# The long convolutions of a hybrid encoder layer: a new order of work, filters through DRAM, an unsplit second stage

## The chip, the cores and the metric

The kernel runs on one core of a Trainium2 chip. A core has TensorE (PE, matmuls), VectorE (DVE), ScalarE (ACT), GpSimd (POOL) and SyncE (SP), which issues most transfers; sixteen DMA engines move data between DRAM and the on-chip SBUF (128 partitions); matmuls write to PSUM, whose banks DVE and ACT empty. The metric is the time of one execution in microseconds of the device, as the median of several runs.

## The reference

One encoder layer on 2048 tokens of 1024 channels, float32. A projection feeds two mixers: a gated long convolution (512 channels) and an RWKV-7 recurrence (512 channels). Their outputs are projected, gated, merged and normed; a SwiGLU network and a second norm follow. What the change touches is the long convolution:

```
u = short_conv3(u, conv_w, conv_b)          # three taps along the tokens
v, x1, x2 = split(u, 3)
h = hyena_filters(L, ...)                   # (L, 2 orders, 2 directions, 512): small network x decaying window
z = x1 * long_conv(v, h[:, 0, 0], h[:, 0, 1], skip[0])
z = x2 * long_conv(z, h[:, 1, 0], h[:, 1, 1], skip[1])

def long_conv(z, h_fwd, h_bwd, d_skip):     # by FFT of length 2L = 4096
    hf = rfft(h_fwd) + conj(rfft(h_bwd))
    return irfft(rfft(z) * hf)[:L] + z * d_skip
```

## The kernel before, in words

The stages follow each other: projection with preparation of the recurrence, the recurrence in 64 steps (`chain`), the convolutions (`hyena`), the merge (`merge`) and the feed-forward network (`ffn`). A scheduler at build time puts each engine's instructions in order by priorities and costs; inside a block under `manual_schedule` the engines named there keep the order of the program. In `chain` and `hyena` of the kernel before only PE is named.

The FFT is done with matmuls against constant matrices, in two stages, for four tiles of 128 channels (index c), twice per tile (order o = 0, 1): eight convolutions i = 2c + o. The steps, with their lines:

- Short convolution (`short`, lines 1166 to 1172): for each 512 tokens one load, one ACT step and two DVE steps. Three per tile: v, x1, x2.
- `turned` (1240): PE transposes of the result to tokens on partitions, copied by ACT.
- `fwd` (1254): the first FFT stage of the data; ACT copies the PSUM tiles into U (1256).
- `flip` (1221): four DVE transposes of 32 x 32 blocks turn U into V, which the second stage needs whole.
- The filters (`filt`): 32 windows (ACT exponentials, 1200), matmuls with the small network's last layer (1201), DVE product with the window (1205), the first FFT stage (1191), an ACT copy (1192), then also a `flip`. The filter of one convolution has 16 matmul pieces, 8 of line 1201 and 8 of line 1191; they are drawn from a generator between other work (`pull`).
- `product`: for q = 0 to 7 the second stage of the filter (`load`, 1275; ACT copy 1281; the two halves swapped by four small SP transfers, 1285), the second stage of the data (`step3`), two DVE products with the filter's spectrum (1312, 1313) and the way back (1297, 1298), copied by ACT (1299). For q above 0 `parts` first splits the data into a high and a low float32r part (ACT 197, DVE 198), and `step3` makes three 512-column matmuls (202 to 204) instead of four fp32 ones.
- After a product: `flip`, `inverse` (1327), for o = 0 a DVE product with x1 (1389) and `fwd` again; for o = 1 `finish`: inverse, ACT copy (1344), PE transposes (1336), DVE product with x2 (1338), a store to `yhd` (1354).

PE in program order goes through tile c as: transposes of x1, finish of tile c - 1, product o = 0 with pieces of the next filter between its rounds, the rest of those pieces, inverse and forward, transposes for tile c + 1, product o = 1, forward of tile c + 1. The first pieces are made at the end of the recurrence, in its last two steps and between its last four small parts. The merge's first half block (`right`) is computed around the last `finish`, after its weights are split.

Of the kernel before, what the change touches and what calls it, by code (L numbers as in the profile page):

```python
# [9 lines left out]
F32 = mybir.dt.float32  # L10
F32R = mybir.dt.float32r
# [178 lines left out]
class Layer:  # L190
# [38 lines left out]
    def build(self):  # L229
        tc, nc = self.tc, self.nc  # L230
        with tc.tile_pool(name="dr", bufs=1, space=DRAM) as dr, tc.tile_pool(name="keep", bufs=1, reuse_waits="tile") as keep:
# [8 lines left out]
            self.Yd = T("Yd", [NCH, P, 256])  # L240
            self.Nd, self.Wd = T("Nd", [2, P, 1024]), T("Wd", [2, P, 1024])
# [377 lines left out]
    def ring(self, k, n=512):  # L619
        return self.cm.tile([P, 514], F32, name="rg", tag=f"rg{k % 14}")[:, 0:n]  # L620

    def chain(self):
# [3 lines left out]
        with tc.tile_pool(name="ch", bufs=1, reuse_waits="tile") as s, tc.tile_pool(name="chp", bufs=1, space=PSUM, reuse_waits="tile") as ps:  # L626
# [166 lines left out]
            def step(n):  # L793
# [16 lines left out]
                if n + 2 < N:  # L810
                    fetch(n + 2)
# [132 lines left out]

            LAST = N - 3
# [81 lines left out]
            with tc.manual_schedule(engines={mybir.EngineType.PE}):  # L1027
# [17 lines left out]
                taps, pieces = iter(()), [1, 2, 3]  # L1045
                self.rush = 0
                for n in range(N):
# [5 lines left out]
                    if n == LAST + 1:  # L1053
                        taps = self.filt(0, 0)
                    if n >= LAST + 1:
                        aux.append(self.part(taps, 4.0))
                        cost += 4.0
# [6 lines left out]
                    if n == LAST:  # L1064
                        self.open()
# [16 lines left out]
                self.taps = taps  # L1082
# [8 lines left out]
    def part(self, gen, need):  # L1091
        while need > 0:
            t = next(gen, None)
            if t is None:
                return
            need -= t
            yield t


    def open(self):  # L1100
# [3 lines left out]
        cu = self.wp.tile([P, 1024], F32, name="cu0", tag="wraw", bufs=2)  # L1104
# [3 lines left out]
        self.turns = dict(cu=0, row=0, w=0, g=0, A=0, B=0, H=0, Hs=0)  # L1108
        self.smalls, self.Vfs = {}, {}
# [6 lines left out]
        self.cus = [cu, self.ring(13, 514)]  # L1116
        self.z0 = self.short(0, True)
# [12 lines left out]
    def next(self, name):  # L1130
        first, n = dict(w=(8, 2), g=(10, 2), A=(12, 2), B=(0, 2), H=(2, 3), Hs=(5, 3))[name]
# [15 lines left out]
    def row(self):  # L1147
        self.turns["row"] += 1
        return self.cm.tile([P, L], F32, name="co", tag=f"X{1 - self.turns['row'] % 2}")


    def short(self, ct, byrest):
        nc, cw, cb = self.nc, self.cw, self.cb
        stt = nc.vector.scalar_tensor_tensor
        o = self.row()
        for b in range(NB):
            u = self.cus[self.turns["cu"] % 2]
            self.turns["cu"] += 1
# [5 lines left out]
            nc.sync.dma_start(u[:, lo:hi], self.ud[ct, :, 512 * b - 1 + lo:512 * b - 1 + hi])  # L1164
            t = self.wp.tile([P, 512], F32, name="cv", tag="ev", bufs=2) if byrest else o[:, 512 * b:512 * b + 512]
# [7 lines left out]
        return o  # L1173

    def pre(self, k):
        return self.cm.tile([P, 32, P], F32, name="U", tag=f"G{k % 2}")


    def filt(self, c, o):
        nc = self.nc  # L1180
        mm = nc.tensor.matmul
        fw4, delta, skip = self.smalls.pop((c, o))
        if (c, o) != (HT - 1, 1):
            self.small(c + o, 1 - o)
        U = self.pre(c)

        def spec(q, g):
            ps, tag, bufs = self.fps
            p = ps.tile([P, 4, P], F32, name="pf", tag=tag, bufs=bufs)
            for j in range(4):  # L1190
                mm(p[:, j], self.Fc[:, 4 * q + j], g[:, j], start=True, stop=True)
            nc.scalar.copy(U[:, 4 * q:4 * q + 4], p)

        for q in range(8):
            win, g = self.next("w"), self.next("g")
            ps, tag, bufs = self.fps
            p = ps.tile([P, 4, P], F32, name="pg", tag=tag, bufs=bufs)
            for j in range(4):
                n = 4 * q + j
                nc.scalar.activation(win[:, j], delta, AF.Exp, scale=self.tcol[:, n:n + 1])  # L1200
                mm(p[:, j], self.H3[:, n], fw4, start=True, stop=n != 0)
                if n == 0:
                    mm(p[:, j], self.e0[0:1], skip[0:1], start=False, stop=True)
            with self.tc.high_priority(offset=2 * FIRST):
                nc.vector.tensor_tensor(out=g, in0=p, in1=win, op=ALU.mult)
            yield 0.87
            if q > 0:
                spec(q - 1, last)
                yield 0.87
            last = g  # L1210
        spec(7, last)
        yield 0.87
        self.Vfs[c, o] = self.flip(U)


    def flip(self, U, ahead=0):
        V = self.hy.tile([P, 32, P], F32, name="V", tag="post", bufs=3)
        for q in range(4):
            sl = slice(32 * q, 32 * q + 32)
            with self.tc.high_priority(offset=ahead):  # L1220
                self.nc.vector.transpose(V[:, :, sl].rearrange("p j c -> p c j"), U[:, :, sl].rearrange("p n c -> p c n"))  # L1221
        return V


    def hyena(self):
        tc, nc, pull = self.tc, self.nc, self.pull
        mm, tt = nc.tensor.matmul, nc.vector.tensor_tensor
        Mc, Fz, Gc = self.Mc, self.Fz, self.Gc
        with tc.tile_pool(name="hy", bufs=1, reuse_waits="tile") as s, tc.tile_pool(name="hyp", bufs=2, space=PSUM, reuse_waits="tile") as ps:
            self.hy = s  # L1230
            self.fps = ps, "pf", 2
            self.cus[1] = self.wp.tile([P, 514], F32, name="cu1", tag="ex")


            def turned(o, z):
                for q in range(4):
                    p = ps.tile([P, 4, P], F32, name="ph", tag="po")
                    for j in range(4):
                        n = 4 * q + j
                        nc.tensor.transpose(p[:, j], o[:, P * n:P * n + P], self.ident)  # L1240
                        yield 0.11
                    with tc.high_priority(offset=FIRST):
                        nc.scalar.copy(z[:, 4 * q:4 * q + 4], p)

            def zt(name):
                return s.tile([P, 16, P], F32, name=name, tag=name, bufs=1)

            def fwd(z, U, q):
                Uv = U.rearrange("p (q b) c -> p b q c", b=2)
                for par in range(2):  # L1250
# [4 lines left out]
                    with tc.high_priority(offset=FIRST):  # L1255
                        nc.scalar.copy(Uv[:, par, 4 * q:4 * q + 4], p)


            def parts(V, q, room):
                v = V[:, 4 * q:4 * q + 4]  # L1260
                if q == 0:
                    return v, None
                k = 4 * (q % 2)
                hi, lo = room[:, k:k + 4], room[:, k + 8:k + 12]
                with tc.high_priority(offset=FIRST):
                    self.split(hi, lo, v)
                return hi, lo

            def step3(hi, lo, q):
# [4 lines left out]
                for j in range(4):  # L1274
                    mm(p[:, j], Mc[:, 0 if 4 * q + j == 0 else 3], hi[:, j], start=True, stop=True)
# [439 lines left out]
```

## Time and profile before

| what | value |
|---|---|
| median of 3 runs | 4029.2 us (4020.6 to 4029.8) |
| the profiled execution | 4030.9 us, its span 4029.1 us |
| mean granted TensorE clock | 0.981 |
| busy PE, DVE, ACT | 3839.9, 2422.1, 1486.7 us |
| from the first spectral product to the end of the convolutions | 1658 to 2174 us of the span |

The profile comes from one execution. A line of a group names the source line, engine, operation, what is written from what, shapes and count, then busy time and the mean of one instruction in ns, then the engine's idle time just ahead of them and what ended it. Names are those of the program's tiles: `rg` are fourteen small buffers used in turn, `pz`, `pq`, `pf`, `po` are the PSUM tiles of the second stage, the way back, the first stage and filters, and the inverse. A matmul of fp32 leaves two records. Matmul ends are modelled, so distances between starts tell PE's pace better than durations.

### The profile page before, as it was taken

How to read it: one execution, taken by the hardware profiler on the slowest of the kernel's cores; microseconds unless marked ns; L12 is line 12 of the kernel's file. 1: busy time of each engine (PE TensorE's matmuls, PEld its weight loads, DVE VectorE, ACT ScalarE, POOL GpSimd, SP SyncE). 2: the span in 40 equal slices, each digit the busy share in tenths (PEclk: the TensorE clock that was granted, in tenths of full speed). 3: DMA queues.
4: the chain of work that ended last, by engine and by line, in shares of the span. 5: the costliest groups of instructions: out<-in, count | busy, mean ns of one | idle time of the engine just before them, and what ended most of it. 6: DMA issues, size and time to landing. Idle time of an engine off the chain costs nothing. (4 is left out here: it accounts for less than half of the span.)

```text
span 4029.1 us, 64417 instructions
## 1 busy us (share of the span) xinstructions
PE 3839.9 (95%) x25872; PEld 3128.8 (78%) x25872; DVE 2422.1 (60%) x3823; ACT 1486.7 (37%) x2912; POOL 93.1 (2%) x139
## 2 busy tenths in 40 slices
PE   8999999899999998898888999999999999999998
PEld 6766557777777777788887899788888877888887
DVE  4456884666667774777876665544444464444444
ACT  3345662333335566665654333211111151111113
POOL 0000001111100000000000000000000000000000
PEclk9999999999999999899999999999999999999999
DMA  4556878676767766221225333411111132111111
GB/s 138 171 166 177 218 201 241 198 214 206 213 202 217 219 195 197 62 72 49 73 71 173 127 123 121 162 48 47 48 47 48 47 130 80 47 48 47 48 47 42
DMA packets 389698, 501.84 MB, mean 125 GB/s; under 512 B 135364, under 2 KB 271053, under 8 KB 388693
## 3 DMA queue, kind: packets, MB, share of 16 engines
q1 hardware_dynamic: 362775, 443.13, 36.7%
q10 hardware_dynamic: 20736, 37.80, 3.1%
q0 software_dynamic: 5888, 16.78, 1.4%
q8 instruction: 204, 3.34, 0.3%
q14 instruction: 95, 0.78, 0.1%
HBM read 352.74 MB, written 127.93 MB: 119 GB/s over the span
## 5 line engine op out<-in xcount | busy, mean ns | idle before, releaser
L202 PE MATMUL acc<-xh,wh 128*128 128x512 f32 x1376 | 580.1, 422 | 10.8 <-ACT xh L197 10.8
L203 PE MATMUL acc<-xl,wh 128*128 128x512 f32 x1376 | 550.1, 400 | 9.8 <-DVE xl L198 9.7
L204 PE MATMUL acc<-xh,wl 128*128 128x512 f32 x1376 | 549.5, 399 | 0.4 <-DVE wl L198 0.4
L1652 DVE TENSOR_TENSOR acc<-pd,acc 128x1024 f32<-128x1024 f32 x320 | 387.7, 1221 | 70.4 <-PE pd L204 64.5
L197 ACT CAST fwh<-raw 128x1024 fp32r<-128x1024 f32 x132 | 138.6, 1050 | 705.6 <-PE pg L203 488.9
L202 PEld LDWEIGHTS acc<-xh,wh 128*128 128x128 f32 x1376 | 261.2, 190 | 125.5 <-issue 48.6
L1680 DVE TENSOR_TENSOR h<-pu,sg 128x512 f32<-128x512 f32 x88 | 60.9, 692 | 492.0 <-PE pu L204 486.0
L203 PEld LDWEIGHTS acc<-xl,wh 128*128 128x128 f32 x1376 | 262.4, 191 | 73.0 <-DVE xl L198 13.6
L204 PEld LDWEIGHTS acc<-xh,wl 128*128 128x128 f32 x1376 | 262.0, 190 | 64.2 <-DVE wl L198 0.8
L202 PE MATMUL pd<-fwh,hh 128*128 128x512 f32 x704 | 276.3, 392 | 2.6 <-DVE acc L1650 2.2
L204 PE MATMUL pu<-fxh,fwl 128*128 128x512 f32 x704 | 277.5, 394 | 0.0
L204 PE MATMUL pg<-fxh,fwl 128*128 128x512 f32 x704 | 277.3, 394 | 0.0
L203 PE MATMUL pg<-fxl,fwh 128*128 128x512 f32 x704 | 276.2, 392 | 0.0
L202 PE MATMUL pg<-fxh,fwh 128*128 128x512 f32 x704 | 276.0, 392 | 0.2 <-DVE fxl L1567 0.2
L202 PE MATMUL pu<-fxh,fwh 128*128 128x512 f32 x704 | 275.3, 391 | 0.4 <-ACT fxh L1566 0.4
L203 PE MATMUL pu<-fxl,fwh 128*128 128x512 f32 x704 | 275.8, 392 | 0.0
L203 PE MATMUL pd<-fwl,hh 128*128 128x512 f32 x704 | 275.5, 391 | 0.0
L204 PE MATMUL pd<-fwh,hl 128*128 128x512 f32 x704 | 274.8, 390 | 0.0
L198 DVE TENSOR_TENSOR fwl<-raw,fwh 128x1024 fp32r<-128x1024 f32 x132 | 161.2, 1221 | 166.4 <-ACT fwh L197 162.5
L198 DVE TENSOR_TENSOR wl<-wraw,wh 128x512 fp32r<-128x512 f32 (+1 forms) x217 | 169.8, 791 | 136.1 <-ACT wh L197 125.0
L197 ACT CAST wh<-wraw 128x512 fp32r<-128x512 f32 (+1 forms) x217 | 150.7, 705 | 235.7 <-PE acc L203 202.3
L1221 DVE STREAM_TRANSPOSE V<-U 128x1024 f32<-128x1024 f32 x96 | 181.0, 1953 | 32.9 <-ACT U L1299 12.5
(299 smaller groups left out, 7583.0 us busy)
## 6 DMA issues: line engine op xcount, KB each, us to landing
wraw<-in_w_in SPq DMA_DIRECT2D x130, 512.0 KB, 5.0
ABp<-ABd SPq DMA_DIRECT2D x64, 512.0 KB, 5.8
raw<-in_fg SPq DMA_DIRECT2D x44, 512.0 KB, 3.4
raw<-in_fu SPq DMA_DIRECT2D x44, 512.0 KB, 3.5
raw<-in_fd SPq DMA_DIRECT2D x44, 512.0 KB, 3.5
ud<-ev ACTq DMA_DIRECT2D x84, 256.0 KB, 3.0
ABd<-AB SPq DMA_DIRECT2D x32, 512.0 KB, 5.0
gated<-ev SPq DMA_DIRECT2D x64, 256.0 KB, 2.8
```

Source lines behind the costliest of these rows:

```text
L197: nc.scalar.copy(hi, src)
L198: nc.vector.tensor_tensor(out=lo, in0=src, in1=hi.bitcast(F32), op=ALU.subtract)
L202: mm(ps, ah, bh, start=start, stop=False)
L203: mm(ps, ah, bl, start=False, stop=False)
L204: mm(ps, al, bh, start=False, stop=stop)
L1221: self.nc.vector.transpose(V[:, :, sl].rearrange("p j c -> p c j"), U[:, :, sl].rearrange("p n c -> p c n"))
L1652: tt(out=acc[t], in0=pf, in1=acc[t], op=ALU.add)
L1680: tt(out=h, in0=put, in1=sg, op=ALU.mult)
```

## The change

- In `hyena` ACT, DVE and SP are also under `manual_schedule`: all engines but POOL take the program's order, and the priorities inside are dropped.
- The program's order is new. The transposes after a product of order 1 are made inside the next tile's first product (`extras`), that tile's `finish` comes after this product; the transposes of the next tile's data are made inside the product of order 1; short convolutions are one stream (`shorts`), one 512-token step at a time, each with its load one step ahead, called from rounds of the products.
- The filters are one stream (`filters`) over all eight convolutions; `upto` and `goals` say how many of the 128 pieces are done by when. A window is made one piece ahead and multiplied in place. The first stage's result is copied into one of two spots, stored by ACT's queue to a DRAM buffer `Hd`, and loaded in the flipped layout by four SP transfers per half filter (`given`). There is no DVE transpose of filters.
- The second stage of the data is four fp32 matmuls for every q (`second`); `parts` and the split matrices are gone.
- At the end of the recurrence the last `fetch` is moved ahead of `open`, which loads what the convolutions need; 5 + 5 pieces are made in its last two steps, and 2, 6, 1 and 0 after its last four parts.
- The merge's weights, gates and inputs are loaded and split inside the last product (`ready`); one ACT tanh covers seven gates.

```
-                if n + 2 < N:
+                if n + 2 < N and n + 2 not in ins:
                     fetch(n + 2)
...
                     if n == LAST:
+                        fetch(n + 2)
                         self.open()
...
-                for part in (gated(2), channel_major(1), channel_major(0), gated(0)):
+                for part, k in ((gated(2), 2), (channel_major(1), 6), (channel_major(0), 1), (gated(0), 0)):
                     self.pull(part, 1e9)
-                    self.pull(taps, 0.8)
+                    self.pull(taps(k), 1e9)
...
+                    u = self.spots[q % 2].rearrange("p (a b) -> p a b", b=P)
+                    nc.scalar.copy(u, p)
+                    nc.scalar.dma_start(self.Hd[c, o, 4 * q:4 * q + 4].rearrange("n p c -> p n c"), u)
...
+                tc.manual_schedule(engines={E.PE, E.Activation, E.DVE, E.SP}):
...
+            def given(i, half):
+                self.upto(16 * i + 16)
+                t = s.tile([P, 16, P], F32, name="Vf", tag=f"vf{half}", bufs=1)
+                for k in range(4):
+                    nc.sync.dma_start(t[32 * k:32 * k + 32], self.Hd[i // 2, i % 2, :, 32 * k + 16 * half:32 * k + 16 * half + 16])
+                Vf[i, half] = t
...
                 for q in range(8):
-                    if q < 6:
-                        hs[q + 2] = load(Vf, q + 2)
-                    H, Hs = hs.pop(q)
-                    p = step3(*zs.pop(q), q)
-                    if q < 7:
-                        zs[q + 1] = parts(Vz, q + 1, room)
+                    p = second(Vz[:, 4 * q:4 * q + 4], q)
+                    H, Hs = hs.pop((i, q))
                     A = self.next("A")
                     B = self.next("B")
-                    with tc.high_priority(offset=FIRST):
-                        tt(out=A, in0=p, in1=H, op=ALU.mult)
-                        tt(out=B, in0=p, in1=Hs, op=ALU.mult)
+                    tt(out=A, in0=p, in1=H, op=ALU.mult)
+                    tt(out=B, in0=p, in1=Hs, op=ALU.mult)
                     AB[q] = A, B
-                    pull(fill, share if q < 7 else 0.0)
+                    n, k = divmod(q + 2, 8)
+                    if i + n < 2 * HT:
+                        load(i + n, k)
+                    self.upto(goals[q])
+                    if q in (1, 5) and i + 1 < 2 * HT:
+                        given(i + 1, q // 4)
                     if q > 0:
                         back(q - 1)
+                    for f in extras.get(q, ()):
+                        f()
                 back(7)
...
+            def goals(i):
+                lead = min(16 * i + 32, 32 * HT)
+                end = min(16 * i + 48 - (6 if i % 2 == 0 else 3), 32 * HT)
+                a = max(self.pieces, lead)
+                return [lead, lead] + [a + (end - a) * (q + 1) // 6 for q in range(6)]
...
+                product(2 * c, Vz, Q, goals(2 * c), extras)
+                VQ, piece = flips(Q)
+                if post:
+                    x2 = self.convs.pop(2 * HT + c - 1)
+                    piece(0)
+                    piece(1)
+                    finish(c - 1, VQ2, x2, lambda q: piece(q + 1) if q in (1, 2) else None)
+                else:
+                    for q in range(4):
+                        piece(q)
+                self.upto(min(self.pieces + 3, 32 * HT))
+                z, U = zt("z"), self.pre()
+                for q in range(6):
+                    if q < 4:
+                        p = inverse(VQ, q)
+                        tt(out=z[:, 4 * q:4 * q + 4], in0=p, in1=x1[:, 4 * q:4 * q + 4], op=ALU.mult)
+                    if q > 1:
+                        fwd(z, U, q - 2)
+                Vz, piece = flips(U)
+                for q in range(4):
+                    piece(q)
...
+                    for q in range(4):
+                        extras[q].append(lambda q=q: piece1(q))
+                    for q in (1, 3, 4, 5, 6, 7):
+                        extras[q].append(conv)
+                    for q in range(4):
+                        extras[6 + q // 2].append(lambda q=q: turn(self.convs[HT + c + 1], x1, q))
+                else:
+                    self.ready(ps, extras)
+                product(2 * c + 1, Vz, Q, goals(2 * c + 1), extras)
+                held = flips(Q)
```

More of the change, by code (lines that the diff above doesn't have):

```diff
@@ L943, in chain, with taps @@
             more, left = columns(), [5.16 * 88]
+            def taps(k):
+                for _ in range(k):
+                    self.upto(self.pieces + 1)
+                    yield 0.87
             LAST = N - 3
@@ L1180, in filt, with filters @@
+    def filters(self):
         nc = self.nc
         mm = nc.tensor.matmul
[L1182 to L1189, printed above, removed]
[L1190 to L1192 removed]
@@ L1194, in filt @@
[L1194 to L1222, printed above, removed]
+        ahead = None
+        def window(delta, q):
+            w = self.next("w")
+            for j in range(4):
+                nc.scalar.activation(w[:, j], delta, AF.Exp, scale=self.tcol[:, 4 * q + j:4 * q + j + 1])
+            return w
```

336 lines of the change are left out of this document (192 added, 144 removed).

## The prediction

> **What bounds the kernel now.** I read the busy line, then windows by stage, TensorE's waits in the convolution stage, and its timeline. First comes the page's busy line; then windows, whose columns are the stretch, its length, busy time (count) of PE, PEld, DVE, ACT, POOL, granted clock, DMA share, GB/s.
>
> ```profile
> PE 3839.9 (95%) x25872; PEld 3128.8 (78%) x25872; DVE 2422.1 (60%) x3823; ACT 1486.7 (37%) x2912; POOL 93.1 (2%) x139
> ```
>
> ```profile
> 1570.00:1658.00 88.00, 60.56 (x585) 54.14 (x584) 55.23 (x91) 63.43 (x156) 0.00 (x0) 0.81 0.46 137
> 1658.00:1792.00 134.00, 117.80 (x996) 109.92 (x996) 105.30 (x119) 77.52 (x164) 0.00 (x0) 0.96 0.22 58
> 1792.00:1926.00 134.00, 119.30 (x1006) 111.06 (x1005) 108.94 (x124) 79.33 (x166) 0.00 (x0) 0.96 0.24 61
> 1926.00:2060.00 134.00, 120.86 (x1020) 112.78 (x1018) 107.76 (x123) 77.99 (x165) 0.00 (x0) 0.96 0.27 73
> 2060.00:2174.00 114.00, 98.08 (x842) 91.67 (x840) 83.29 (x102) 52.66 (x107) 0.00 (x0) 0.97 0.30 84
> ...
> 2150.00:2174.00 24.00, 20.48 (x196) 18.68 (x194) 16.07 (x18) 7.50 (x17) 0.00 (x0) 1.00 0.27 86
> ```
>
> Over the whole kernel PE is the bound. The convolutions are the exception: from the first spectral product to their end lie 3 x 134 + 114 = 516 us, four tiles of 128 channels. VectorE is busy 79 to 81% in the first three. Three of PE's waits there (us, times, longest), and the loop inside a product:
>
> ```profile
> PE pz L1275 <- DVE V L1221: 14.4, 4, 6.0
> ...
> PE pg L1201 <- DVE rg L1205: 8.0, 11, 1.4
> ...
> PE pz L202 <- DVE rg L1313: 4.7, 3, 1.6
> ```
>
> ```profile
> 1928.35 1.06 PE L1275 MATMUL pz<-V,Mc 128*128 128x128 f32 x8
> 1929.16 0.47 PE L202 MATMUL pz<-vh,Ms 128*128 128x512 f32 x1
> ...
> 1929.93 1.05 PE L1201 MATMUL pg<-fw,H3b 128*128 128x128 f32 x8
> 1930.82 0.39 PE L1297 MATMUL pq<-rg,Mc 128*128 128x128 f32 x2
> ...
> 1932.61 1.06 PE L1275 MATMUL pz<-V,Mc 128*128 128x128 f32 x8
> ```
>
> Inside a product PE runs without a gap. A "quad" (four fp32 matmuls into one PSUM tile, 8 records) takes 0.89 us from start to start (1929.93 to 1930.82), the two quads of the way back 1.79, one round 4.26. So time is lost between products, where PE waits for DVE's transposes (line 1221).
>
> **The change, part by part.** Engine prices, busy in total and mean ns of one, and three transfers (ns on the issuing queue, or KB and us to landing):
>
> ```profile
> L1221 DVE STREAM_TRANSPOSE V<-U 128x1024 f32<-128x1024 f32 x96 | 181.0, 1953 | 32.9 <-ACT U L1299 12.5 <-ACT U L1256 11.5 <-ACT U L1192 8.7
> ...
> L1200 ACT ACTIVATE rg<-delta,k_c_tcol 128x128 f32<-128x128 f32 x245 | 83.8, 394 | 33.0 <-DVE rg L1205 32.8
> ...
> L1312 DVE TENSOR_TENSOR rg<-pz,rg 128x512 f32<-128x512 f32 x64 | 43.9, 687 | 45.3 <-PE pz L204 35.9 <-PE pz L1275 9.4
> ...
> L1205 DVE TENSOR_TENSOR rg<-pg,rg 128x512 f32<-128x512 f32 x62 | 42.1, 680 | 18.3 <-PE pg L1201 9.4 <-ACT U L1192 4.6 <-ACT rg L1200 3.6
> L198 DVE TENSOR_TENSOR vh<-V,vh 128x512 fp32r<-128x512 f32 x56 | 38.2, 690 | 0.5 <-ACT vh L197 0.5
> L1281 ACT COPY rg<-pz 128x512 f32<-128x512 f32 x64 | 37.2, 584 | 30.1 <-PE pz L1275 19.8 <-DMA rg<-rg 7.8 <-DVE rg L1312 2.3
> ...
> L197 ACT CAST vh<-V 128x512 fp32r<-128x512 f32 x56 | 33.7, 616 | 28.9 <-DVE V L1221 22.0 <-PE pz L204 6.0
> L1172 DVE SCALAR_TENSOR_TENSOR co<-cu,k_conv_w,cv 128x512 f32<-128x512 f32 x28 | 30.0, 1114 | 0.4 <-DMA yhd<-co 0.2
> ...
> L1166 ACT ACTIVATE cv<-cu,k_conv_b,k_conv_w 128x512 f32<-128x512 f32 x28 | 22.5, 812 | 12.5 <-DMA cu<-ud 12.4
> ...
> L1338 DVE TENSOR_TENSOR co<-pv,co 128x512 f32<-128x512 f32 x16 | 17.6, 1167 | 0.5 <-PE pv L1336 0.5
> ```
>
> ```profile
> L345 ACTq DMA_DIRECT2D ud<-ev x84: 326/326/1523, 21.6 to 643.7; - x84
> ```
>
> ```profile
> L1285 SPq DMA_DIRECT2D rg<-rg x256: 507/588/1959, 1650.2 to 2145.4; - x128
> ```
>
> ```profile
> yrd<-yo SPq DMA_DIRECT2D x16, 256.0 KB, 2.7
> ```
>
> Unsplit second stage: 56 DVE subtracts (38.2 us) and 56 ACT casts (33.7) go; on PE three 512-column matmuls become a quad, a round of 4.26 becomes five quads, 4.45, so +0.19 x 56 = +10.6 us where PE is the bound. Filters through DRAM: 32 of the 96 DVE transposes go (62 us). In their place stand 64 stores issued by ACT (0.33 us each as the row of ud, at most 0.6 as SP's row, 21 to 38 us, beside PE since ACT has 55 free in each 134) and 64 loads on SP. SP's queue then holds per round four swaps of halves (4 x 0.59 = 2.35), a convolution input and, twice a product, four loads (2.35), under 5.5 us of a round of 5.3 to 6.2; a swap has two rounds until its reader. All this is hidden.
>
> What counts is PE's work in its new order and what it cannot cover. Prices of the other PE steps, by start to start:
>
> ```profile
> 1906.50 5.37 PE L1254 MATMUL pfz<-z,Fz 64*128 64x128 f32 x48 [0.17 <-ACT U L1256]
> 1911.80 2.05 PE L1275 MATMUL pz<-V,Mc 128*128 128x128 f32 x16
> 1913.78 1.97 PE L1327 MATMUL po<-V,Gc 128*64 128x128 f32 x32
> 1915.68 0.66 PE L1336 MATMUL pv<-k_c_ident,rg 128*128 128x128 f32 x4
> 1916.27 1.09 PE L1327 MATMUL po<-V,Gc 128*64 128x128 f32 x16
> ```
>
> A forward step (16 records) 5.30/3 = 1.77, an inverse step 0.95, four transposes about 0.5. A middle tile (c = 1, 2): even product 8 + 8 + 16 quads and 13 filter pieces = 45 quads = 40.0; finish of the tile before, 4 x (0.95 + 0.5) = 5.8; 3 pieces 2.7; inverse and forward 4 x (0.95 + 1.77) = 10.9; the next tile's transposes and forward 8.9; odd product 48 quads and 4 sets of transposes 44.5. Sum 112.8. Tile 0 has 3 pieces fewer and no finish: 104.4. Tile 3 has 3 pieces in its even product (31.2), 30 quads in its odd one (26.7), finish 5.8, 10.9: 74.6. The end stays at 24, the last window above.
>
> Stalls in this order: after an even product DVE ends a short convolution (about 1 us) and, 0.8 us after the last matmul, makes four transposes, 7.8 us, that the inverse needs. Tile 0 covers that 9.6 with 2.7: stall 6.9. Tiles 1 and 2 have two of finish's products (2 x 1.17) in DVE's order before the last transpose, 11.9, against 8.5 of cover: 3.4, and about 2 more where finish's other two products stand ahead of the gating and the ACT copies run behind: 5.4. Tile 3: 11.9 - 5.8 = 6.1, 1, and its second set of transposes with no cover, 8.6: 15.7. So 111.3 + 2 x 118.2 + 90.3 + 24 = 462, of which 33 stalls. By the same prices the 516 of now hold 14.2 more for 16 pieces that the change makes earlier and 10.6 less for the split stage, 408 of work and the end's 24, so 84 are lost.
>
> Program order on ACT, DVE and SP: a short convolution's two DVE steps (up to 1.11 each) now stand ahead of the next round's two products (0.69 each), and wait for ACT's 0.81, itself behind four exponentials (83.8/245 = 0.34 each) and copies (0.58). The products end about 2.5 us late, but PE needs them one round later, so mostly nothing; the nearest row, 1.6 us per wait (pz after line 1313), gives 0 to 8 us per product. I take 1, nearer the gapless loop: 8.
>
> The granted clock: 0.96, three times, and 0.97 leave 0.04 x 402 + 0.03 x 114 = 19.5 us below full rate. It drops after a wait:
>
> ```profile
> 1722.46 2.05 PE L1275 MATMUL pz<-V,Mc 128*128 128x128 f32 x8 [3.06 <-DVE V L1221]
> ```
>
> A quad's records took 2.05 us there against 1.06 above. With fewer waits I take 12, bounds 5 and 20. The Trainium skill (TensorE: Matmul & The Clock Gate, "Why this matters for your kernels") advises against PE gaps above about 3 us, since the clock then halves until some 3.4 us of work have passed; this speaks against a change that gathers its waits into few long ones. The trace agrees with it in the row just shown; six stalls of over 3 us at 1.7 us each would be an estimate of 10 by that page instead of my 12.
>
> Stage: 462 + 8 + 12 = 482, against 516: -34.
>
> Start of the stage (tail of the recurrence before 1658):
>
> ```profile
> 1585.44 1.12 PE L786 MATMUL pT<-k_c_ident,BK 128*128 128x128 f32 x4 [6.18 <-DMA BK<-ABd]
> ```
>
> ```profile
> 1580.29 0.56 SPq L754 DMA_DIRECT2D BK<-ABd  x1
> ```
>
> ```profile
> 1600.00:1620.00 20.00, 12.87 (x132) 11.38 (x132) 9.41 (x20) 19.63 (x59) 0.00 (x0) 0.91 0.13 38
> ```
>
> The last fetch is moved ahead of the stage's own loads on SP, so this 6.2 us wait goes. Next late is ACT, full from 1600 on, which gets windows, copies and stores for 5 more pieces (about 7 us) before the stage begins and, until product 0, 13 pieces (6.5 x (4 x 0.34 + 0.58 + 0.33) = 14.8) besides copies. I expect product 0 to begin 3 us earlier with 32 pieces done instead of 16, which the sum for tile 0 already uses; bounds -12 (the wait and half of ACT's load go) and +8 (all on the path).
>
> After the stage:
>
> ```profile
> 2164.27 6.56 SPq L1486 DMA_DIRECT2D wr<-in_w_hy  x2
> 2173.33 0.34 SPq L1354 DMA_DIRECT2D yhd<-co  x1
> ```
>
> The merge's first weight loads were issued 9 us ahead of the last store; with SP in program order they follow it. 0 to +9, I take +4, since PE has other work for part of it.
>
> Sum: -34 - 3 + 4 = -33. The profiled execution took 4030.9 (span 4029.1), so 3998; the median of the runs, 4029.2, lies 1.7 below it, so 3996.
>
> **The rivals.** (1) Slower: the DRAM buffer Hd. If a store must wait until an earlier read of Hd has landed, ACT stands still at each of the 16 reads for their four issues and landing, 2.35 + 2.7 = 5 us; with two PSUM buffers of each kind PE runs on for about two quads, 1.8, so 16 x 3 = +48: 4044. It decides once a store waits longer than its spot's reuse, two pieces' spacing (some 10 us in a product). For it: Hd is one tensor, read and written in turns. Against: so is ud, and its 84 stores show a median equal to the least, 326 ns, so no usual wait. (2) No change: the program order costs 5 us per product instead of 1, three waits of 1.6: +32, 4028. For it: those waits exist now, when DVE and ACT may still pick their order. Against: all three engines beside PE have a fifth or more free in every round. (3) A larger gain: start -12, nothing for order, clock 5, merge 0: -33 - 9 - 8 - 7 - 4 = -61, 3968. For it: DVE loses 100 of some 405 us in the stage, so stalls behind it may shrink more than I count.
>
> **How the numbers follow.** Forecast 0.60 (its own range 3975 to 4016), rival 1 0.09, rival 2 0.12, rival 3 0.19. Some 12 us, 0.3%, are what this kernel's measurement can tell. Forecast and rival 3 lie below 4017: faster 0.79; rival 2: same 0.12; rival 1: slower 0.09. The range, 3952 to 4030, takes in rivals 2 and 3 with their bounds and leaves out rival 1.
>
> **What would show it.** Right: the middle tiles at about 123 us each; TENSOR_TENSOR on vh gone; 64 transposes instead of 96; rounds of 4.45 us or more without gaps; no wait for BK; PE's waits in the stage mostly for transposes after even products and before the last product. Wrong: waits on pz or pf inside products (rival 2), ACT idle ahead of stores or exponentials with DMA as releaser (rival 1), product 0 well after 1658, or the merge starting with a wait of more than 9 us for its weights.

## The result and the profile after

| | before | after |
|---|---|---|
| median of four runs | 4029.5 us (4020.6 to 4032.2) | 4059.8 us (4057.8 to 4065.8) |
| the profiled execution, its span | 4030.9, 4029.1 us | 4057.8, 4056.0 us |
| from the first transposes of the data to the last store of the convolutions | 1629.5 to 2173.3: 543.8 us | 1632.9 to 2205.1: 572.2 us |
| the rest of the span | 3485.3 us | 3483.8 us |

The change makes the kernel slower, by a little under one per cent: 1.0082 of the time before, 95% interval 1.0063 to 1.0100. The forecast was 3996. In the two profiles all of the difference lies inside the convolutions; the rest of the span is 1.5 us shorter. (In the profiles of this study the stage begins anywhere from 1629 to 1643 us with the same program ahead of it, so I compare the stage by its own length and the kernels by medians.)

The windows of the two stages, before and after, with the columns as in the prediction:

```profile
1629.50:2173.30 543.80, 478.37 (x4007) 445.90 (x4005) 427.51 (x486) 303.47 (x630) 0.00 (x0) 0.96 0.26 68
```

```profile
1632.90:2205.10 572.20, 490.90 (x4246) 467.13 (x4245) 360.53 (x404) 269.75 (x563) 0.00 (x0) 0.92 0.46 121
```

VectorE and ACT lost the work that they were to lose (427 to 361, 303 to 270 us), and TensorE still waits more: busy 491 of 572 us, at a clock of 0.92 instead of 0.96, with nearly twice the traffic (121 GB/s instead of 68). TensorE's and ACT's waits in the stage after (us, times, longest):

```profile
PE pv L1368 <- DVE co L1370: 13.5, 6, 2.9
PE po L1358 <- DVE V L1289: 13.0, 3, 7.0
PE pfz L1280 <- ACT U L1281: 12.0, 1, 12.0
PE pz L1295 <- ACT rg L1311: 11.1, 7, 4.6
PE pz L1295 <- DVE rg L1338: 10.9, 10, 1.4
PE pz L1295 <- DVE V L1289: 9.0, 1, 9.0
```

```profile
ACT cv L1173 <- DMA cu<-ud: 42.7, 14, 11.8
...
ACT co L1173 <- DMA cu<-ud: 17.5, 7, 5.1
```

```profile
ACT cv L1166 <- DMA cu<-ud: 12.4, 9, 3.7
...
ACT co L1166 <- DMA cu<-ud: 7.7, 10, 1.7
```

The last fence is ACT before. ACT waits 60 us for the inputs of the short convolutions instead of 20. ACT is now in program order, so copies that TensorE needs stand behind each such wait. Why the inputs are late is seen in SP's timeline after, at the start of the stage and inside the first product:

```profile
1634.48 3.65 SPq L1305 DMA_DIRECT2D Vf<-Hd  x8
1638.47 13.98 SPq L1163 DMA_DIRECT2D cu<-ud  x4
...
1709.46 2.43 SPq L1305 DMA_DIRECT2D Vf<-Hd  x4
1711.98 0.38 SPq L1163 DMA_DIRECT2D cu<-ud  x1
1712.48 6.72 SPq L1315 DMA_DIRECT2D rg<-rg  x4
1719.30 0.53 SPq L1163 DMA_DIRECT2D cu<-ud  x1
```

The input that is asked for at 1638.47 stands behind eight filter loads of 256 KB and ends ACT's wait of 11.83 us at 1647.17. At 1712.48 four swaps, 2.41 us where nothing holds them, take 6.72, right behind four filter loads, and the next input waits behind them. ACT's copies of the ways back in this first product, at most 5.36 us apart until then, lie 9.17 and 8.59 us apart (1703.87, 1713.04, 1721.63).

### The profile page after: what moved, and what is told of

The parts are those of the page before. It is cut to its first block, busy times and chain, and to the rows that moved or that the text cites. A ratio compares the mean times of both kernels' runs of the same rounds, so it can differ in the third digit from the quotient of the medians.

```text
span 4056.0 us, 64933 instructions
## 1 busy us (share of the span) xinstructions
PE 3851.7 (95%) x26152; PEld 3151.0 (78%) x26152; DVE 2350.6 (58%) x3734; ACT 1459.1 (36%) x2853; POOL 93.0 (2%) x139
## 4 chain that ended last, share of the span: by engine, by line
PE 50%; DMA 3%; DVE 3%; ACT 2%; SPq 1%; issue 1%; DVEq 0%; ACTq 0%
PE pg L202 4%; PE pg L204 4%; PE pu L202 4%; PE pg L203 4%; PE pu L203 4%; PE pu L204 4%; PE pd L202 4%; PE pd L204 4%; PE pd L203 4%; PE pz L1295 2%; PE pm L204 1%; PE pm L202 1%; PE pm L203 1%; DMA cu<-ud 1%; PE po L202 1%; PE po L203 1%
## 5 line engine op out<-in xcount | busy, mean ns | idle before, releaser
L202 PE MATMUL acc<-xh,wh 128*128 128x512 f32 x1376 | 577.9, 420 | 10.4 <-ACT xh L197 10.4
L202 PEld LDWEIGHTS pd<-fwh,hh 128*128 128x128 f32 x704 | 132.0, 187 | 40.6 <-DVE acc L1745 5.4
```

The source lines that it names most:

```text
L202: mm(ps, ah, bh, start=start, stop=False)
```

## The experiments

Each was timed beside the kernel before on the same chip; ratios are to that. Differences between two versions are between medians, in part from different chips, on which the kernel before took 4026.7 to 4029.8 us; differences of some 4 us and less are not told apart. The experiments stand in the order of the argument.

**The second stage alone, in the kernel before.**

```
-                if q == 0:
+                if q >= 0:
                     return v, None
```

> The kernel before with one part of the change alone: the second stage of the data is four fp32 matmuls for every q, the split into two float32r parts is left away (the tiles and the split matrix stay allocated). Price of the prediction: +0.19 us in each of 56 rounds, +10.6 us where TensorE is the bound, so 4040. Rival: VectorE and ScalarE lose 72 us of work, and the waits for transposes that stood behind them shrink by as much or more: 4020 to 4030.

Measured: 4047.6 us, ratio 1.0049 (1.0032 to 1.0066), so 13 to 27 us slower, about 19. The price per round was too low in that order. TensorE stands still in the stage for hardly longer than before (68.0 us against 65.4), but it is busy 504.5 instead of 478.4 us, and its clock falls from 0.96 to 0.93:

```profile
1630.70:2203.20 572.50, 504.54 (x4288) 477.47 (x4286) 394.49 (x431) 271.58 (x575) 0.00 (x0) 0.93 0.24 65
```

The work taken from ACT and VectorE gave nothing back, so the rival falls for the old order.

**The same part, undone in the changed kernel.**

```
-                    p = second(Vz[:, 4 * q:4 * q + 4], q)
+                    p = step3(*zs) if q else second(Vz[:, 0:4], 0)
...
+                    zs = parts(q + 1) if q < 7 else None
```

> The changed kernel with one part undone: the second stage of the data is split into two float32r parts again for q above 0 (cast on ACT, subtract on VectorE one round ahead, in program order), three 512-column matmuls instead of four fp32 ones. Theory A (the unsplit stage costs TensorE the same here as it did in the kernel before, 19 us instead of the priced 10.6): 4060 falls to 4035 to 4047. Theory B (in program order the casts stand behind the late conv inputs and TensorE waits for them): within 6 us of 4060, with new waits of the second stage for the split.

Measured: 4073.3 us, ratio 1.0103 (1.0081 to 1.0125): 13.5 us slower than the changed kernel, the other way round than in the old order. That is theory B's mechanism, at more than the 6 us that it allowed. The row that decides is a new wait of the second stage for its split:

```profile
PE pz L203 <- DVE vh L198: 21.6, 17, 2.7
```

Casts and subtracts that stand one round ahead in program order come too late. So in this order the unsplit stage gains, and "+10.6" was no property of the part alone. Whether the split placed further ahead would be in time was not tried.

**Only TensorE in program order.**

```
-                tc.manual_schedule(engines={E.PE, E.Activation, E.DVE, E.SP}):
+                tc.manual_schedule(engines={E.PE}):
```

> The changed kernel with one part undone: in the convolutions only TensorE keeps the program's order, and ACT, VectorE and SP are ordered by the planner again (without the priorities that the change dropped). Theory A (program order on SP and ACT costs the waits for conv inputs): the planner asks for the inputs earlier, ACT's waits for them fall to about the 20 us of the kernel before, and the time falls by 15 to 25 us. Theory B (what costs is the work and the uncovered transposes, or the planner's order is worse without priorities): 4055 or more.

Measured: 4072.4 us, ratio 1.0105 (1.0079 to 1.0132). ACT's waits for the inputs do fall, to 24 us, as theory A had it, but the time rises by 12.6: theory B. TensorE then waits for what the planner puts late:

```profile
PE pz L1295 <- DVE rg L1338: 16.8, 11, 3.3
PE pf L1217 <- DVE rg L1235: 16.4, 6, 2.9
```

The planner ran here without the priorities that the change dropped, so this compares the program order with that planner only; against it the program order gains. What is lost must then lie in something in the order.

**The filter loads moved at the start.**

```
-            for h in range(2):
-                given(0, h)
...
                     conv()
+                if q == 3:
+                    for h in range(2):
+                        given(0, h)
```

> The changed kernel, but the eight loads of the first two half filters are issued behind the four short-convolution steps at the start of the convolutions instead of ahead of them. Theory A (a conv input stands behind 1 MB of filter loads on the queue, and ACT, in program order, stands behind that input): the 12.0 us wait of the forward matmuls for ACT's copy goes to under 3 us, the first spectral product begins 7 to 12 us earlier than at 1677, and the time falls by 7 to 12 us to about 4050. Theory B (the start is late because sixteen more filter pieces are made before it, and the wait only shows where): the wait moves to the filter's loads or to the copies of the pieces, the time stays within 3 us of 4060.

Measured: 4059.8 us, ratio 1.0074 (1.0052 to 1.0096): no gain. The 12 us wait goes to 2.6, and another takes its place:

```profile
PE pz L1295 <- DMA Vf<-Hd: 5.3, 1, 5.3
PE pfz L1280 <- ACT U L1281: 2.6, 1, 2.6
```

Two kinds of loads are needed at nearly the same time; their order on one queue only chooses who waits. The stage is 3 us shorter, and this can't be told apart in the time.

**The inputs asked for one round earlier.**

```
-            nxt = given(k + 1) if k + 1 < len(seq) else None
...
-            u = nxt
+            u, nxt = nxt, given(k + 2) if k + 2 < len(seq) else None
```

> The changed kernel, but each short-convolution input is asked for at the end of the step that frees its buffer instead of at the beginning of the next step: about one round of a product (5 us) earlier, same two buffers. Theory A (the program order couples ACT to inputs that are asked for one step ahead and land 4 to 9 us later): ACT's waits for these inputs fall from 60 us to under 20, the waits of the second stage for ACT and DVE (11.1 and 10.9 us) to under half, the time falls by 15 to 25 us to about 4040. Theory B (these waits of ACT are slack, and what costs is the waits of the transposes and the work itself): ACT's waits for inputs fall too, but the time stays within 5 us of 4060.

Measured: 4038.9 us, ratio 1.0014 (0.9999 to 1.0028): 21 us less than the changed kernel, inside theory A's range. ACT's waits fall from 60 to 26.6 us, not below 20: the one of 10 us at the start stays. The second stage's waits fall to 8.3 us for ACT and 7.6 for VectorE, not to half.

**The merge's inputs earlier in the last product.**

```
+                    def early():
+                        self.wraws = [self.weights_raw("r", dt) for dt in range(2)]
+                    extras[6].append(early)
...
-        extras[4].append(branch)
+        extras[3].append(inputs)
+        extras[5].append(branch)
```

> The changed kernel, but in the last product the recurrence's input of the merge is asked for in round 3 and split in round 5 (before: both in round 4), and the first two weight loads of the merge are asked for at the end of the seventh product instead of in round 0 of the eighth. Theory A (the last product takes 50 us instead of 29 because ACT waits, in program order, for transfers that were only just asked for): ACT's waits of 7.4 and 4.7 us go, the last product takes 8 to 13 us less, the time falls by 8 to 13 us to about 4049. Theory B (the last product is long because the throttle grants less clock after the 9 us wait ahead of it and because its casts are too much work for ACT and DVE): less than 4 us.

Measured: 4053.8 us, ratio 1.0059 (1.0039 to 1.0080): 6 us less, between the two theories. The two waits of ACT in the changed kernel's last product are gone:

```profile
ACT y L197 <- DMA yraw<-yrd: 7.4, 1, 7.4
...
ACT wh L197 <- DMA wr<-in_w_rw: 4.7, 1, 4.7
```

The 9.0 us wait for transposes ahead of it and the late conv inputs of its first rounds are not.

**The three together.**

> The three edits of the other runs together: filter loads behind the first conv steps, conv inputs one round earlier, the last product's inputs earlier. Theory A: the savings add to 28 to 45 us, so 4015 to 4032, about the kernel before the change or a little less. Theory B: the time stays above 4045.

Measured: 4033.7 us, ratio 1.0013 (1.0000 to 1.0026): 26 us less, just outside theory A, far from B. The stage takes 541.8 us.

**The recurrence's last fetch alone, in the kernel before.**

```
+                    if n == LAST:
+                        fetch(n + 2)
                         self.open()
```

> The kernel before with the last fetch of the recurrence moved ahead of the loads of the convolutions. If the wait of 6.2 us for BK is on the path: it goes and the time falls by 4 to 6 us, to about 4024. If ACT, full from there on, is what is late next: less than 2 us.

Measured: 4025.0 us, ratio 0.9995 (0.9979 to 1.0011): no difference that can be told, and the time alone does not part the two cases (4 to 6 us or under 2). The 6.18 us wait for BK is gone; by the trace ACT is late next. TensorE's waits there are then for ACT:

```profile
1595.82 0.33 PE L878 MATMUL pgt<-k_c_ident,y 128*128 128x128 f32 x1 [4.43 <-ACT y L870]
...
1616.68 0.48 PE L878 MATMUL pgt<-k_c_ident,y 128*128 128x128 f32 x1 [3.24 <-ACT y L870]
```

**More pieces as cover, and the first filter's halves apart.**

```
-                self.upto(min(self.pieces + 3, 32 * HT))
+                self.upto(min(self.pieces + 6, 32 * HT))
...
+                if q in (1, 3):
+                    given(0, q // 2)
```

> The three earlier edits together, and two more: the first half filter is loaded behind the second conv step of the start and the second half behind the fourth, and six filter pieces instead of three stand between each even product and the inverse (the next product then starts with none of its own). Theory A (the middle of a tile waits for transposes that nothing covers, and the start waits for 1 MB of loads): the wait of 7.0 us for the filter falls to under 3, and the waits after even products (8.0 in the first tile) fall by 2.7 us in each of three tiles: 10 to 13 us less than with the three edits, about 4022. Theory B (the pieces only move a wait): within 4 us of 4034.

Measured: 4027.2 us, ratio 0.9998 (0.9983 to 1.0014): 6.5 us less than the three edits, about half of what theory A gave. The waits for transposes after even products fall from 14.4 to 6.7 us and the one for the filter goes, but those of the second stage for VectorE's products grow from 7.6 to 11.1. With the split put back on top of it (the edit of the second experiment):

> The kernel with the three earlier edits and six pieces after even products, and the split second stage put back. Theory A: 10 to 20 us less than without the split, 4007 to 4017, faster than both kernels. Theory B (VectorE and ACT get their 72 us of work back, in program order, and TensorE waits for them): within 5 us of 4027.

Measured: 4036.2 us, ratio 1.0013 (0.9997 to 1.0029), 9 us slower than without the split: theory A falls again, and the split costs more than the 5 us of theory B.

**Where the transposes' tiles lie.** They take longer after the change, and so does everything that stands behind them. The group after:

```profile
L1289 DVE STREAM_TRANSPOSE V<-U 128x1024 f32<-128x1024 f32 x64 | 140.9, 2229 | 29.2 <-ACT U L1281 24.0 <-ACT U L1330 5.1
```

Three versions with 64 bytes of padding in SBUF: ahead of the tiles of the recurrence and the convolutions (on the version with six pieces), ahead of those that the transposes write (on the same version), and the latter alone in the changed kernel. The line is that of the last two.

```
+            s.tile([P, 16], F32, name="pad", tag="pad", bufs=1)
```

> The same as the run with six pieces, and 64 bytes of padding ahead of the convolutions' tiles in SBUF. The transposes took 1.95 us before and 2.23 after the change; the tiles that they read lay at 0 modulo 128 bytes before and at 64 after, the tiles that they write at 64 in both. With the padding both lie at 0. If the place of what is read decides: 1.95 us per transpose, and 4 to 8 us less time. If the two tiles' place against each other decides (before 64 bytes apart modulo 128, after none, here none), or the transfers beside them: 2.23 us still and no change of time.

> The kernel with the three earlier edits and six pieces, and 64 bytes of padding ahead of the tiles that the transposes write, so that they lie at 0 modulo 128 bytes and what is read at 64 (before the change: written at 64, read at 0; after: both at 64; in the run with padding ahead of all: both at 0, and 2.22 us). If the two tiles' place against each other decides: 1.95 us per transpose, and 3 to 8 us less than 4027. If it does not: 2.23 us and no change; then transfers beside them, or another difference, stay as causes.

> The changed kernel with nothing but the 64 bytes of padding ahead of the tiles that the transposes write. Theory A (the place of the tiles, an accident of the change, costs it 0.28 us in each of 64 transposes, uncovered in five places of four): transposes of 1.95 us, the waits of 13.0, 9.0 and 13.5 us for transposes and what stands behind them each about 1 to 3 us shorter, the time 4 to 8 us less than 4060. Theory B: transposes of 1.95 us, but hidden behind the late inputs: less than 3 us.

Measured: 4024.3 us, ratio 0.9992 (0.9973 to 1.0010); 4022.6, 0.9975 (0.9962 to 0.9988); and 4052.6, 1.0058 (1.0040 to 1.0075), 7 us less than the changed kernel. The transposes of the first two:

```profile
L1289 DVE STREAM_TRANSPOSE V<-U 128x1024 f32<-128x1024 f32 x64 | 140.3, 2221 | 28.3 <-ACT U L1281 23.2 <-ACT U L1330 5.1
```

```profile
L1290 DVE STREAM_TRANSPOSE V<-U 128x1024 f32<-128x1024 f32 x64 | 123.4, 1956 | 28.3 <-ACT U L1282 23.2 <-ACT U L1331 5.1
```

Neither the place of what is read decides nor the traffic, which is the same: it is the place of the two tiles against each other. In the changed kernel the shorter transposes are worth 7 us, theory A; its three waits fall to 11.8, 7.9 and 10.4 us.

**The filter loads on another queue.** The same edit three times: on the changed kernel alone, on the fastest version so far, and there together with the next edit.

```
-                    nc.sync.dma_start(t[32 * k:32 * k + 32], self.Hd[...])
+                    nc.gpsimd.dma_start(t[32 * k:32 * k + 32], self.Hd[...])
```

> The changed kernel with one edit: the 64 loads of the filters are issued by GpSimd's queue, which does nothing else in the convolutions, instead of SP's. Theory A (the failed step is that SP's queue hides its work: four loads that wait for stores and for their buffer stand ahead of conv inputs and swaps, and ACT and VectorE, in program order, stand behind those): ACT's waits for conv inputs fall from 60 to under 35 us, the 12.0 us wait of the start goes or shrinks, and the time falls by 15 to 30 us, to 4030 to 4045. Theory B (the filter loads only add to waits that the one-step lead of the inputs makes anyway): 10 us or less.

Measured: 4025.7 us, ratio 0.9998 (0.9981 to 1.0015). One edit takes 34 us away, more than theory A's range, and with it all that the change had lost. The stage, then ACT's waits for the inputs:

```profile
1642.20:2180.50 538.30, 481.59 (x4246) 460.69 (x4244) 360.79 (x404) 270.64 (x562) 29.23 (x61) 0.94 0.49 128
```

```profile
ACT co L1173 <- DMA cu<-ud: 10.3, 6, 4.6
ACT cv L1173 <- DMA cu<-ud: 10.1, 5, 6.7
```

60 us of waits have become 20, without asking for anything earlier. The transfers themselves, KB and median us to landing, in the changed kernel and here:

```profile
Vf<-Hd SPq DMA_DIRECT2D x56, 256.0 KB, 4.9
cu<-ud SPq DMA_DIRECT2D x21, 256.5 KB, 4.9
```

```profile
Vf<-Hd POOLq DMA_DIRECT2D x64, 256.0 KB, 6.1
...
cu<-ud SPq DMA_DIRECT2D x21, 256.5 KB, 3.6
```

An input lands in 3.6 instead of 4.9 us, although the same bytes move; the filter loads, which have time, take longer, and so do the swaps (3.3 instead of 2.5). The copies of the ways back in the first product lie 5.36 us apart where they were 9.17 and 8.59. The Trainium skill (DMA: Bandwidth & Descriptors, "Issuing engines are not separate DMA queues") says that issuing from several engines only saves the sequencer's time, usually small; here the edit is worth 34 us, since others stand behind that sequencer and the edit changes more than its time (the next section has it). The same page ("Queues, rings and completion order") has each engine take a queue's descriptors in order and share itself out among queues, packet by packet; the shorter landing of the inputs agrees.

> The fastest version so far (three earlier edits, six pieces, padding; 4022.6), with the loads of the filters issued by GpSimd's queue instead of SP's. Theory A (SP's program order lets swaps and conv inputs stand behind four loads that wait): VectorE's waits for swaps fall from 12.2 us to under 4, ACT's for conv inputs below 10, and the time falls by 4 to 10 us. Theory B (what is late is the landing, with 1 MB of loads on the same sixteen engines, whoever issues them): waits as before, within 3 us of 4022.

Measured: 4008.2 us, ratio 0.9942 (0.9921 to 0.9963), 14 us less than the version that it is made from, more than theory A gave. VectorE's waits for swaps fall from 12.2 to 4.7 us and ACT's for conv inputs from 24.4 to 11.0, both not quite as far as theory A said.

**Pieces inside the finish, and both.**

```
+                        if q in (2, 3):
+                            self.upto(min(self.pieces + 2, 32 * HT))
```

> The fastest version so far, with four of the six filter pieces moved in between the steps of the finish, ahead of the transposes that wait for VectorE. Theory A (TensorE waits there 11.2 us for VectorE's products, with work at hand that stands behind): the waits for transposes of the finish fall to under 5 us, the time falls by 4 to 8 us. Theory B (VectorE is the bound of this stretch, 4 transposes and 4 products): the wait moves to the inverse, less than 3 us.

> Both edits: filter loads on GpSimd's queue and four pieces inside the finish. Theory A of both: 8 to 18 us less than 4022.6, so 4005 to 4015. Theory B of both: within 4 us of 4022.

Measured: 4019.8 us, ratio 0.9981 (0.9966 to 0.9995), and 4005.7, ratio 0.9939 (0.9918 to 0.9960). The first is 3 us less, theory B: the waits for transposes of the finish fall from 11.2 to 3.2 us, and 7.1 us appear as waits of a piece for VectorE. Both together give the lowest time, 0.6% below the kernel before the change; it is not told apart from the queue's edit alone. Its stage:

```profile
1633.60:2148.60 515.00, 473.64 (x4246) 453.45 (x4244) 344.84 (x404) 271.94 (x563) 28.99 (x60) 0.96 0.50 133
```

## Why the prediction was wrong, point by point

**The step that failed: "All this is hidden", said of SP's queue.** It was a sum of issue times, 5.5 us per round against rounds of 5.3 to 6.2, and a sum of that kind has no room for standing still: four swaps, priced at 2.35 us, take 6.16 to 8.40 in six of the seven rounds that load the second half of a filter. SP's order puts filter loads, swaps and conv inputs behind each other, and ACT and VectorE, in program order too, stand behind those. Moving the 64 loads off this queue gives 34 us, asking for the inputs earlier 21. These two are not independent and don't add; each by itself shows the place. Of the 64 us between forecast and result, runs of one edit on the changed kernel give 34 for the queue, 7 for the tiles' place and 6 for the merge's inputs; these need not add either, and the rest is not parted.

What makes SP stand can be read off the program and the trace. After the change the profile names stores to Hd as what SP waited for, also ahead of swaps:

```profile
SPq L1315 <- DMA Hd<-rg: 15.4, 6, 4.6
SPq L1315 <- DMA Hd<-cu: 15.3, 3, 6.1
SPq L1140 <- DMA Hd<-cu: 13.1, 3, 5.2
```

A swap needs no store of Hd, and the pause at 1712.48 lies in the midst of four swaps that need the same things. But the program, as built, counts the landings of SP's and ACT's transfers with eight counters in turn, and each of these transfers waits until the last one on its counter, eight places before it, has landed. GpSimd's transfers have counters of their own. At 1712.48 the third swap shares its counter with a filter load and the fourth with ACT's store to Hd. The trace agrees: that store lands 7.3 us after its issue, and only then is the fourth swap issued.

```profile
1711.41 0.39 ACTq L1220 DMA_DIRECT2D Hd<-cu  x1
```

```profile
1718.69 0.51 SPq L1315 DMA_DIRECT2D rg<-rg  x1
```

So SP's swaps hang on long loads and on another engine's stores that they have nothing to do with. With the loads on GpSimd's queue nothing stands behind them on SP, and they take no places among the eight counters; of the swaps' waits for Hd 5.1 us are left. The inputs also land sooner. How the 34 us fall to these three no run tells.

**Rival 1** looked at the right buffer and the wrong end. ACT, which issues the stores, waits 0.6 us for them in the whole stage; it is SP that waits for stores and loads, and what stands behind these on SP that is late. Its 4044 was nearer to the result than the forecast, by the wrong mechanism.

**Rival 2** (waits inside products) describes what the waits look like: second stage for ACT 11.1 and VectorE 10.9 us. Its cause, ACT and VectorE in program order, is not enough by itself: with that order kept and the loads on another queue, 34 us go. The planner's order is no remedy, at 12.6 us slower. **Rival 3** (VectorE's lighter load shrinks the stalls behind it) is not seen: the stalls that it shares in stayed.

**The unsplit second stage, +10.6.** Measured 19 in the old order and -13.5 in the new one. The step took the price of a round and left out who has to make the split, and when.

**Transposes, 1.95 us each.** They took 2.23, by the place of the tiles: 7 us. The trace of before could not show this.

**The stalls** were right. After the first product 6.9 us were forecast and 7.04 measured, ahead of the last one 8.6 and 9.00, and beside the three finishes 16.9 (5.4, 5.4 and 6.1) against the row of 13.5 us for TensorE's transposes behind VectorE's products, even with slower transposes. What came on top is 12.0 at the start, 11.1 and 10.9 inside products. With the loads on the other queue these are 6.7, 9.1 and 3.3, and of the 9.1 us 8.1 are two waits in the last product, which has no filter loads.

**The last product, 26.7 us of work,** took 48.5 (2131.03 to 2179.58). TensorE stands still for 11.9 of them, mostly because ACT waits for the merge's inputs and the conv inputs; the rest is matmuls at a mean granted clock of 0.83. The working had no transfer of this product in it; that they are hidden was the failed step again. Asking for the merge's inputs earlier gives 6 us of it.

**The start.** Product 0 was to begin 3 us earlier, at 1655; it began at 1677. The wait for BK went, as said. The 12 us wait for the conv input was not seen, and moving the filter loads alone only changed who waits.

**The clock** was to lose 12 us in the stage, 20 at most. At 0.92 of 572 it loses 46, so this term was mis-sized too. By windows of 2 us some 16 of the 46 fall while TensorE stands still (0.57 from 2122.1 to 2131.0), so in part these are the waits once more; the other 30 compare with 21 before. With the loads on the other queue the sum is 32 (0.94 of 538), in the fastest version 21 (0.96 of 515). After the wait of 9.00 us the matmuls run at half speed for some 5 us:

```profile
2131.03 2.07 PE L1295 MATMUL pz<-V,Mc 128*128 128x128 f32 x8 [9.00 <-DVE V L1289]
2132.89 1.91 PE L1295 MATMUL pz<-Vf,Mc 128*128 128x128 f32 x8
2134.60 2.02 PE L1295 MATMUL pz<-V,Mc 128*128 128x128 f32 x8
2136.41 1.31 PE L1295 MATMUL pz<-Vf,Mc 128*128 128x128 f32 x8
```

That agrees with the prediction's reading. Short waits do it too: after waits of 0.57 and 1.41 us two quads from 1713.52 on take 1.75 and 1.70. But waits are not all: the unsplit stage in the old order lowered the clock to 0.93 with hardly more of them. What else lowers it stays open.

**A middle tile,** forecast at 123 us, takes 131 from one store of a result to the next (1866.75 to 1997.92), in the fastest version 120 (1841.05 to 1961.45). A small misreading is in the sum: four transposes were put at 0.45 to 0.5 us, where the row shown has 0.59 (1915.68 to 1916.27), some 1.5 us per tile.

**What was right:** the merge costs no more than its lower bound of 0, where 4 was taken (behind the stage 1855.8 us have become 1850.9), rounds of 5.36 us without gaps where no transfer is late, 64 transposes and no split. The work itself was sized well: with the queue, the inputs' times, the tiles' place and the covers mended the stage takes 515 us, where the forecast for this stretch was 543.8 - 34 - 3 = 507. The changed order can do nearly what was said of it; the kernel as changed could not.

## What to carry to other kernels

A queue in program order is priced by what stands behind its slowest entry, not by the sum of its issue times: list for each transfer who reads it next, how long before it is asked for, and what stands ahead of it that may wait. To what it waits for belongs what the build adds: here the transfer eight places before it, from another engine too. Before an engine is put into program order, give transfers that have time (here whole filters) another queue than those that are read one step later. And price an edit in the order in which it will stand: the same unsplit stage cost 19 us in one order and saved 13.5 in another.

## What was not expected of the hardware

- The same VectorE transpose of 128x1024 fp32 takes 1.95 us when the tile that it reads and the tile that it writes lie, by the program's allocation, 64 bytes apart modulo 128 (read at 0 and written at 64, or the reverse: 1.953 and 1.956), and 2.22 to 2.23 when both lie at the same place (both at 64, or both at 0). In the slow builds the two addresses differ by multiples of 4096 bytes, so a larger modulus than 128 fits as well. Other VectorE steps show nothing of the kind: the products of the second stage take 0.68 us in all of them.
- GpSimd's queue issued a 256 KB load in 0.49 us (mean) and landed it in 6.1 (median), against medians of 0.42 and 4.9 on SP's; for loads with a whole product of time this costs nothing.
- Four fp32 matmuls in place of three of 512 columns in two float32r parts cost 0.19 us by the trace's distances and, in the old order, 19 us in 56 rounds, 0.34 each, with a granted clock of 0.93 instead of 0.96.
